# Weight preparation spread over a whole up-projection, five early loads, and a pending convolution in six steps

## The chip, the core and the metric

The kernel is one program on one core of a Trainium2 chip. The core has a matrix engine (TensorE, PE in the profile; its weight loads are the row PEld), VectorE (DVE), ScalarE (ACT), GpSimd (POOL), and SyncE (SP), whose queue issues nearly all transfers between the chip's memory (DRAM) and the on-chip buffers (SBUF). Matrix products are accumulated in PSUM, which DVE and ACT read. Each engine works through its own list of instructions in order, and waits on semaphores for the others. The metric is the time of one execution on the device in microseconds (us).

## What is computed

One layer on 2048 tokens of width 1024 in float32: an input projection, sparse indexed attention beside a pooling mixer, gates, an output projection, a layer norm, then the gated MLP that this study is about, and a second layer norm. The MLP, cut from the reference:

```python
D_MODEL, SEQ, D_FF, CONV_WIDTH = 1024, 2048, 2816, 3

def conv_ffn(x, conv_w, conv_b, w_up, w_down):
    h = x @ w_up
    h = lax.conv_general_dilated(h, conv_w[:, None, :], window_strides=(1,),
                                 padding=[(CONV_WIDTH - 1, 0)],
                                 dimension_numbers=('NWC', 'WIO', 'NWC'),
                                 feature_group_count=2 * D_FF) + conv_b
    gate, val = jnp.split(h, 2, axis=-1)
    return (jax.nn.silu(gate) * val) @ w_down

# in reference(), after the first layer norm:
ffn = conv_ffn(x, conv_w[l], conv_b[l], w_ffn_up[l], w_ffn_down[l])
x = layer_norm(ALPHA * x + ffn, ln2_g[l], ln2_b[l])
```

## The kernel before

**Arithmetic.** A float32 operand is split into a high part that the matrix engine takes as it is and a low part, the remainder. `mm3` then makes three matmuls of every product: high by high, high by low, low by high. The two big products of the MLP are made as 2 x 2 blocks by a scheme with seven block products instead of eight, so both operands are first added up into seven combinations, and the seven results are added up into the four blocks.

**Stages.** The program runs through projections, attention, the output projection with the first layer norm, and then `ffn`: `up_half(0)`, `down_half(0)`, `up_half(1)`, `down_half(1)`, one pair for each half of the tokens (1024). Work that is written out between two matmuls is put among the engines' lists by a scheduler, by the program's order and by what is ready.

**Up.** `up_half` has NF = 22 units, two for each of 11 channel groups (gate, then value). A unit makes seven products in the order ORDER, so a half has 154; each is 12 matmuls of 128x512. `evacuate` adds the results into the tiles h1 and h2. `conv` returns the causal convolution of a unit as six pieces (0 to 5): 0 and 1 are the three taps for h2, 2 and 3 for h1, and 4 and 5 (`hidden`) multiply value by gate and store two of the combinations for the down projection to DRAM (the tensors h). Each unit runs the pieces of the unit before it, one before each product; those of the last unit are left in `self.pending`. `hidden(1)` also queues five sums (`total`) in `self.hsum`; `self.hsum.pop(0)()` runs one at a time, and each is stored in h. They run on DVE in the first half, on POOL in the second.

**Weights of the up projection.** `up_weights` is a generator of 154 steps. A step makes one of the seven combinations of a unit's weights (a sum on POOL, except for two of seven; a high part by ACT; a low part on POOL) and stores it to DRAM (`uw`), at 512 KB. The first 98 steps (W_BEFORE = 14 units) run during attention. `up_more` runs the other 56 inside `up_half(0)`: W_RATE steps are credited for each product. `up_fetch` reads each weight back UP_AHEAD = 5 products before its use, in both halves. Stores go through `store`, which issues them a product or two later (`turn`). Stores and fetches are issued by SP, in one order.

**Down.** `down_half` makes seven products in the order DOWN, each of NP = 11 steps over p; a step is 4 row blocks of 3 matmuls of 128x512. Its operands are read by `down_load` (h from DRAM and one or two blocks of the weight, 256 KB each) and prepared by `down_split` (a sum on POOL where there are two blocks, the high part on ACT, the low part on DVE, or half on POOL). `loaded` and `split` count how far these are; a step splits two steps ahead and loads up to three further. `down_ahead` makes the first loads and splits inside the last unit of `up_half`. In the first steps, `down_half` runs the pending convolution and then the queued sums, and reads eight tiles of x. `lastk` holds the last steps of a product back and makes them row block by row block, so that `collect` (DVE, from PSUM) can start on the first block while PE does the others.

## Time and profile before

| | us |
|---|---|
| median of three timed runs | 3335.93 (3323.9 to 3339.29) |
| the profiled execution | 3325.95 |
| its span, from the first instruction to the last | 3324.2 |

The profile is of one execution. Its span is 1.75 us shorter than that execution's own time. In the trace, `up_half(0)` runs from about 1945 us to 2411 us, the down half after it to about 2640 us, the second up half to about 3090 us and the second down half to the end.

A row of a view by stretch gives the time from the start of the span, its length, and for each engine its busy time and, in brackets, how many instructions ran; then the granted clock of PE (1.00 is full speed), the mean busy share of the 16 DMA engines, and the rate in GB/s. In a view of waits, "A <- B: total, times, longest" says that engine A stood idle until B had released it. In a row of the timeline, the first two numbers are start and length, and in brackets at the end stands the idle time before it and what ended that. Names are the program's: b a large SBUF tile, m a half-size one, p PSUM, uw the prepared weights in DRAM, h the hidden combinations in DRAM, l a tile of the late pool. SPq is SP's queue, where a row is the issue of a transfer. Nearly every operation is recorded on the one line (L150) of a wrapper; of SP's lines, L363 is a store, L1471 a fetch of a weight, L1448 a load of raw up weights, L1617 and L1627 the loads of the down half, L1599 a store of h that is issued at once.

### The profile page before, as it was taken

To read this page: it belongs to the slowest core of one execution; us is meant where nothing else is said; L and a number is where in the kernel's file an instruction comes from. 1 tells how busy PE (TensorE), PEld (TensorE's weight loads), DVE (VectorE), ACT (ScalarE), POOL (GpSimd) and SP (SyncE) were. 2 spreads that over 40 slices of the span, in tenths; PEclk is the share of its full clock that TensorE was granted. 3 is DMA by queue.
4 is the path that set the end of the run, shared out by engine and by line. 5 is a ranking of instruction groups with operands and counts; after the bars stand their busy time and mean duration, and the time that the engine had idled before them with its cause. 6 is when DMAs were issued, how large, how long until landed. Compare 5 with 4: busy or idle time off the path is not lost. (4 is left out here: it accounts for less than half of the span.)

```text
span 3324.2 us, 46905 instructions
## 1 busy us (share of the span) xinstructions
PE 3168.4 (95%) x15918; PEld 2658.2 (80%) x15918; DVE 2423.5 (73%) x4475; ACT 1585.2 (48%) x2854; POOL 1271.3 (38%) x1302
## 2 busy tenths in 40 slices
PE   8998899999999899999999989999989999999898
PEld 8887688888898778888878877777868778888687
DVE  5589878996899887777676576666578765555597
ACT  3465737855678566666621133333244432223343
POOL 3139400010010787667731154550066511211684
PEclk9999899999999999999999999999999999999999
DMA  8457755754566344443464458997697665666884
GB/s 323 146 197 279 246 210 186 249 198 145 189 249 224 120 162 173 143 158 145 149 231 161 157 209 319 348 328 278 226 356 273 206 250 221 235 248 244 314 308 167
DMA packets 325679, 745.71 MB, mean 224 GB/s; under 512 B 30074, under 2 KB 115006, under 8 KB 325438
## 3 DMA queue, kind: packets, MB, share of 16 engines
q1 hardware_dynamic: 315646, 724.88, 60.8%
q10 hardware_dynamic: 9792, 17.83, 1.4%
q8 instruction: 126, 2.06, 0.3%
q14 instruction: 115, 0.94, 0.1%
HBM read 514.36 MB, written 228.23 MB: 223 GB/s over the span
## 5 line engine op out<-in xcount | busy, mean ns | idle before, releaser
L150 PE MATMUL p<-b,b 128*128 128x512 f32 (+3 forms) x12644 | 2785.6, 369 | 79.5 <-ACT b L150 20.6
L150 PEld LDWEIGHTS p<-b,b 128*128 128x128 f32 x12644 | 2173.6, 191 | 484.0 <-ACT b L150 23.1
L150 ACT ACTIVATE b<-p 128x512 fp32r<-128x512 f32 (+9 forms) x726 | 428.7, 612 | 667.9 <-PE p L150 628.1
L150 ACT ACTIVATE b<-b 128x1024 fp32r<-128x1024 f32 (+2 forms) x248 | 253.2, 1027 | 397.7 <-POOL b L150 148.9
L150 DVE TENSOR_TENSOR b<-b,b 128x1024 fp32r<-128x1024 f32 (+5 forms) x246 | 358.6, 1488 | 78.9 <-ACT b L150 75.9
L150 ACT ACTIVATE m<-b,F 128x448 bf16<-128x448 f32 (+3 forms) x448 | 366.1, 820 | 84.2 <-DVE F L150 67.3
L150 DVE TENSOR_SCALAR_CACHE_REDUCE m<-b,F 128x512 bf16<-128x512 f32 (+6 forms) x476 | 370.8, 808 | 17.8 <-DMA q<-m 12.4
L150 POOL TENSOR_TENSOR b<-b,b 128x256 fp32r<-128x256 f32 (+3 forms) x276 | 315.9, 1161 | 72.3 <-ACT b L150 66.2
L150 DVE TENSOR_TENSOR m<-m,p 128x512 f32<-128x512 f32 x176 | 120.5, 685 | 245.2 <-ACT b L150 207.0
L150 POOL TENSOR_TENSOR b<-b,m 128x512 f32<-128x512 f32 x110 | 196.7, 1808 | 237.9 <-DMA b<-h 165.3
L150 POOL TENSOR_TENSOR m<-b,b 128x512 f32<-128x512 f32 x99 | 144.4, 1466 | 349.4 <-issue 258.4
L150 DVE SCALAR_TENSOR_TENSOR b<-b,cw,b 128x1023 f32<-128x1023 f32 (+1 forms) x176 | 243.4, 1385 | 35.7 <-ACT b L150 34.5
L150 POOL TENSOR_SCALAR b<-b 128x256 fp32r<-128x256 f32 (+3 forms) x216 | 117.3, 558 | 379.4 <-DMA b<-in_w_in_dram 127.7
L150 PE MATMUL p<-b 128*128 128x512 f32 x616 | 235.8, 399 | 13.2 <-ACT b L150 8.7
L150 DVE TENSOR_TENSOR b<-p,b 128x512 fp32r<-128x512 f32 (+1 forms) x286 | 201.5, 713 | 59.5 <-ACT b L150 57.2
L150 PE MATMUL p<-ident,b 128*128 128x128 f32 x1456 | 214.8, 277 | 20.9 <-ACT b L150 14.4
L150 DVE CUSTOM_DVE_ANT_0 b<-p,b 128x1024 f32<-128x1024 f32 (+7 forms) x192 | 173.9, 908 | 67.4 <-PE p L150 66.1
L150 PEld LDWEIGHTS p<-ident,b 128*128 128x128 f32 x1456 | 176.6, 142 | 53.5 <-ACT b L150 17.5
L150 ACT ACTIVATE b<-b,mx 128x1024 f32<-128x1024 f32 (+7 forms) x192 | 171.6, 896 | 67.2 <-DVE mx L150 63.0
L150 DVE SCALAR_TENSOR_TENSOR b<-b,ws,b 128x768 f32<-128x768 f32 (+5 forms) x154 | 157.4, 1050 | 43.1 <-ACT b L150 41.0
L150 ACT ACTIVATE m<-p 128x512 f32<-128x512 f32 (+1 forms) x180 | 105.4, 593 | 152.9 <-PE p L150 136.9
L150 PE MATMUL p<-kst,b 128*128 128x384 f32 (+3 forms) x656 | 151.6, 361 | 4.5 <-DVE b L150 3.3
(126 smaller groups left out, 2386.7 us busy)
## 6 DMA issues: line engine op xcount, KB each, us to landing
b<-uw SPq DMA_DIRECT2D x308, 512.0 KB, 6.8
b<-wp SPq DMA_DIRECT2D x192, 512.0 KB, 6.2
uw<-l SPq DMA_DIRECT2D x98, 512.0 KB, 2.9
b<-in_w_ffn_down_dram SPq DMA_DIRECT2D x154, 256.0 KB, 5.4
b<-h SPq DMA_DIRECT2D x154, 256.0 KB, 5.4
wp<-b SPq DMA_DIRECT2D x64, 512.0 KB, 5.6
uw<-b SPq DMA_DIRECT2D x56, 512.0 KB, 5.4
h<-m SPq DMA_DIRECT2D x110, 256.0 KB, 5.6
```

The costliest lines, as they stand in the source:

```text
L150: return f(*args, **kw)
```

## The change

There are four edits, in numbers and in an index. W_RATE goes from 0.6 to 0.42: the 56 steps of weight preparation take 56/0.42 = 133 products instead of 56/0.6 = 93. DOWN_AHEAD = 5 loads (three before) and four splits (two before) are made in the last unit of each up half, from its third product on instead of its fifth. The pending convolution is run one piece in each of the first six steps of the down half, in the order 0, 1, 4, 2, 3, 5, instead of two pieces in each of three steps. In the sixth product of the first down half, three steps are held back instead of two.

```diff
--- before.py
+++ after.py
@@ -79,7 +79,8 @@
 W_PLAIN = {3: 0, 4: 3}
 W_SUMS = {2: (2, 3, OP.add), 1: (0, 3, OP.add), 6: (2, 0, OP.subtract), 5: (0, 1, OP.add), 7: (1, 3, OP.subtract)}
 UP_AHEAD = 5
-W_BEFORE, W_FROM, W_RATE = 14, 4, 0.6
+W_BEFORE, W_FROM, W_RATE = 14, 4, 0.42
+DOWN_AHEAD = 5
 DOWN = (4, 2, 1, 3, 6, 5, 7)
 H_PLAIN = {3: (0, 0), 4: (1, 1)}
 H_SUMS = {1: ((0, 0), (1, 1), OP.add), 2: ((0, 1), (1, 1), OP.add), 5: ((0, 0), (1, 0), OP.add),
@@ -1582,8 +1583,8 @@
                 else:
                     product(i, banks[BANK[m]], m, range(4))
                     evacuate(m, banks[BANK[m]], st)
-                if u == NF - 1 and s >= 4:
-                    self.down_ahead(hf, s - 4)
+                if u == NF - 1 and s >= len(ORDER) - DOWN_AHEAD:
+                    self.down_ahead(hf, s - len(ORDER) + DOWN_AHEAD)
                 yield 2.7
             pending = conv(st, n % 2, u // 2)
         self.pending = pending
@@ -1660,7 +1661,7 @@
         NP = NF // 2
         total = len(DOWN) * NP
         gb = self.load_norm("ln2_g", "ln2_b")
-        loaded, split = 3, 2
+        loaded, split = DOWN_AHEAD, DOWN_AHEAD - 1
         ys, fresh = {}, set()
 
         def product(acc, p, r, part):
@@ -1684,7 +1685,7 @@
                 t = [self.PS2([P, 2, G]) for _ in range(2)]
                 acc = [t[0][:, 0], t[0][:, 1], t[1][:, 0], t[1][:, 1]]
             final = hf == 1 and mi == len(DOWN) - 1
-            lastk = LASTK if final else 2 if hf == 0 and mi in (4, 5) else 0
+            lastk = LASTK if final else 2 if hf == 0 and mi == 4 else 3 if hf == 0 and mi == 5 else 0
             held = []
             for p in range(NP):
                 i = mi * NP + p
@@ -1698,9 +1699,8 @@
                 if loaded < min(split + 3, total):
                     self.down_load(hf, loaded)
                     loaded += 1
-                if mi == 0 and p < 3:
-                    self.pending[2 * p]()
-                    self.pending[2 * p + 1]()
+                if mi == 0 and p < 6:
+                    self.pending[(0, 1, 4, 2, 3, 5)[p]]()
                 elif self.hsum:
                     self.hsum.pop(0)()
                 if mi == 0 and 1 <= p <= 8:
```

The instructions are the same in kind and number on every engine; only their order changes. Three places show it. The first is SP's list in the middle of `up_half(0)`, from the fetch of weight 61 (uw_14179) to that of weight 67 (uw_14185). Rows b<-uw are fetches, rows uw<-b stores of prepared weights, h<-b is a store of h. Before:

```order
L1471 DMA b_23812<-uw_14179 128x1024
L1471 DMA b_23834<-uw_14180 128x1024
L363 DMA uw_14249<-b_23814 128x1024
L1471 DMA b_23853<-uw_14181 128x1024
L1471 DMA b_23877<-uw_14182 128x1024
L363 DMA uw_14250<-b_23855 128x1024
L1471 DMA b_23899<-uw_14183 128x1024
L363 DMA uw_14251<-b_23879 128x1024
L1471 DMA b_23918<-uw_14184 128x1024
L363 DMA h_186<-b_23817 128x512
L1471 DMA b_23941<-uw_14185 128x1024
L363 DMA uw_14252<-b_23920 128x1024
```

With the change:

```order
L1472 DMA b_23748<-uw_14179 128x1024
L1472 DMA b_23767<-uw_14180 128x1024
L1472 DMA b_23790<-uw_14181 128x1024
L364 DMA uw_14239<-b_23769 128x1024
L1472 DMA b_23810<-uw_14182 128x1024
L364 DMA uw_14240<-b_23812 128x1024
L1472 DMA b_23833<-uw_14183 128x1024
L1472 DMA b_23852<-uw_14184 128x1024
L1449 DMA b_23854<-in_w_ffn_up_dram 128x4x256
L1449 DMA b_23855<-in_w_ffn_up_dram 128x4x256
L364 DMA h_186<-b_23750 128x512
L1472 DMA b_23879<-uw_14185 128x1024
```

Between the same fetches stand two stores of weights instead of four, and the weights stored are ten earlier ones (121 and 122 instead of 131 to 134).

The second is SP's list at the last unit of `up_half(0)`, just behind the last fetches. Rows with in_w_ffn_down_dram are weight blocks for the down half (m: the second block of a sum), b<-h the hidden operand of the same load, h<-m the stores of sums of the hidden tiles. Before:

```order
L1471 DMA b_25700<-uw_14270 128x1024
L1471 DMA b_25722<-uw_14271 128x1024
L363 DMA h_236<-m_25724 128x512
L363 DMA h_247<-m_25744 128x512
L1617 DMA m_25800<-in_w_ffn_down_dram 128x512
L363 DMA h_258<-m_25764 128x512
L1617 DMA m_25820<-in_w_ffn_down_dram 128x512
L1617 DMA m_25843<-in_w_ffn_down_dram 128x512
L1617 DMA m_25861<-in_w_ffn_down_dram 128x512
L1617 DMA m_25871<-in_w_ffn_down_dram 128x512
L1617 DMA b_25799<-in_w_ffn_down_dram 128x512
L1627 DMA b_25799<-h_183 128x512
```

With the change:

```order
L1472 DMA b_25722<-uw_14271 128x1024
L364 DMA h_214<-m_25702 128x512
L1618 DMA b_25763<-in_w_ffn_down_dram 128x512
L1628 DMA b_25763<-h_183 128x512
L364 DMA h_236<-m_25724 128x512
L1618 DMA m_25764<-in_w_ffn_down_dram 128x512
L1618 DMA m_25789<-in_w_ffn_down_dram 128x512
L364 DMA h_247<-m_25744 128x512
L1618 DMA m_25815<-in_w_ffn_down_dram 128x512
L364 DMA h_258<-m_25769 128x512
L1618 DMA b_25788<-in_w_ffn_down_dram 128x512
L1628 DMA b_25788<-h_184 128x512
```

The first load's tile (b_25763) and its h now stand ahead of the stores h_236, h_247 and h_258, while before (b_25799) they stood behind them; the second load (b_25788) stands where the first stood before.

The third is DVE's list at the start of `down_half(0)`. Rows with cw are taps of the pending convolution, a TENSOR_TENSOR of 128x1024 from two other tiles is the low part of a split (or, where it writes its own first input, the product of value and gate), and m<-b,b is a queued sum. Before:

```order
L150 TENSOR_TENSOR b_25796<-m_25741,p_6505_25699 128x512
L150 TENSOR_TENSOR b_25867<-b_25842,b_25866 128x1024
L150 SCALAR_TENSOR_TENSOR b_25875<-b_25781,cw_22028,b_25875 128x1023
L150 SCALAR_TENSOR_TENSOR b_25875<-b_25781,cw_22028,b_25875 128x1022
L150 TENSOR_TENSOR b_25899<-b_25860,b_25898 128x1024
L150 TENSOR_TENSOR b_25875<-b_25875,b_25704 128x1024
L150 SCALAR_TENSOR_TENSOR b_25907<-b_25796,cw_22028,b_25907 128x1023
L150 TENSOR_TENSOR b_25928<-b_25870,b_25927 128x1024
L150 SCALAR_TENSOR_TENSOR b_25907<-b_25796,cw_22028,b_25907 128x1022
L150 TENSOR_TENSOR b_25907<-b_25907,b_25746 128x1024
L150 TENSOR_TENSOR b_25956<-b_25892,b_25955 128x1024
L150 TENSOR_TENSOR m_25964<-b_25907,b_25875 128x512
```

With the change:

```order
L151 TENSOR_TENSOR b_25869<-b_25839,b_25868 128x1024
L151 SCALAR_TENSOR_TENSOR b_25885<-b_25786,cw_22028,b_25885 128x1023
L151 SCALAR_TENSOR_TENSOR b_25885<-b_25786,cw_22028,b_25885 128x1022
L151 TENSOR_TENSOR b_25885<-b_25885,b_25704 128x1024
L151 TENSOR_TENSOR b_25923<-b_25862,b_25922 128x1024
L151 TENSOR_TENSOR b_25949<-b_25880,b_25948 128x1024
L151 SCALAR_TENSOR_TENSOR b_25957<-b_25811,cw_22028,b_25957 128x1023
L151 SCALAR_TENSOR_TENSOR b_25957<-b_25811,cw_22028,b_25957 128x1022
L151 TENSOR_TENSOR b_25976<-b_25900,b_25975 128x1024
L151 TENSOR_TENSOR b_25957<-b_25957,b_25746 128x1024
L151 TENSOR_TENSOR b_26002<-b_25926,b_26001 128x1024
L151 TENSOR_TENSOR m_26034<-b_25957,b_25885 128x512
```

The same six pieces are run ahead of the first queued sum. By then six splits had had their low part before, and now eight; the pieces of the two tiles (b_25885 and b_25957, before b_25875 and b_25907) have two splits between them, where before they followed each other directly.

## The prediction

> **What bounds the kernel now.** I began with the page's first part: the span, and who is busy in it.
>
> ```profile
> span 3324.2 us, 46905 instructions
> PE 3168.4 (95%) x15918; PEld 2658.2 (80%) x15918; DVE 2423.5 (73%) x4475; ACT 1585.2 (48%) x2854; POOL 1271.3 (38%) x1302
> ```
>
> PE is busy for 95%, so the end is set by PE's work, and a change that adds or removes no matmul (this one only moves work) can gain only where PE waits or runs at a low clock. The share is a mean over stages, so I next asked for busy times by stretch: the first up half while weights are still prepared, the rest of that half, the start of the first down half, then its middle, and the same pair for the second down half.
>
> ```profile
> core 0: us, PE busy (x) PEld busy (x) DVE busy (x) ACT busy (x) POOL busy (x), PEclk, DMA share, GB/s
> 1990.00:2260.00 270.00, 251.59 (x1045) 200.08 (x1046) 169.47 (x166) 93.81 (x151) 135.84 (x85) 0.96 0.94 338
> 2260.00:2405.00 145.00, 145.00 (x633) 117.61 (x632) 91.49 (x107) 43.68 (x60) 0.00 (x0) 1.00 0.63 233
> 2405.00:2475.00 70.00, 61.52 (x246) 45.95 (x246) 49.55 (x45) 26.98 (x28) 35.00 (x22) 0.98 0.94 343
> 3085.00:3155.00 70.00, 60.90 (x245) 47.36 (x244) 44.89 (x43) 26.76 (x26) 45.74 (x28) 0.95 0.91 326
> 3155.00:3300.00 145.00, 145.00 (x641) 120.10 (x640) 127.26 (x120) 66.17 (x70) 102.83 (x58) 1.00 0.76 265
> ```
>
> The number in brackets behind PE counts matmuls, so each row gives a pace. Undisturbed, the up half takes 145/633 = 0.229 us for one, or 2.75 us for a product of 12, and the down half 145/641 = 0.226 us. At these paces 1045 matmuls need 239.4 us of the first row's 270: **30.6 us are lost** while weights are prepared. The down starts need 55.6 and 55.4 of 70: **14.4 and 14.6 us** are lost. These three places hold nearly all that the change can touch.
>
> **Part 1: weight preparation at 0.42 steps for a product instead of 0.6.** Nothing is removed: 56 steps now take 133 products instead of 93, of 154. What ended PE's longest waits in the first row's stretch, what was transferred there (issues, size, us to landing), and whom the issuing queue (SP) waited for:
>
> ```profile
> PE p L150 <- DMA b<-uw: 14.0, 7, 4.6
> b<-uw SPq DMA_DIRECT2D x90, 512.0 KB, 6.8
> uw<-b SPq DMA_DIRECT2D x50, 512.0 KB, 5.4
> h<-m SPq DMA_DIRECT2D x30, 256.0 KB, 5.6
> b<-in_w_ffn_up_dram SPq DMA_DIRECT2D x12, 512.0 KB, 7.9
> h<-b SPq DMA_DIRECT2D x12, 256.0 KB, 6.3
> SPq L363 <- POOL b L150: 122.1, 42, 8.2
> ```
>
> PE waits seven times for a fetched weight (b<-uw). Two things make fetches late. First, bytes: 152 transfers of 512 KB (0.524 MB) and 42 of 256 KB are 90.7 MB; in 1045/12 = 87 products that is 1.043 MB each, which at 2.75 us a product asks for 380 GB/s, while the row shows 338 delivered at a DMA share of 0.94. 1.043 MB at 338 GB/s takes 3.09 us, just the pace seen (270/87 = 3.10). Second, order: SP issues in order and stood 122 us, 42 times, at a weight store whose POOL result was not ready, with fetches queued behind it. One such case, in order of time:
>
> ```profile
> 2058.16 0.62 SPq L1471 DMA_DIRECT2D b<-uw  x1
> 2067.05 0.32 SPq L363 DMA_DIRECT2D uw<-b  x1
> ...
> 2067.94 0.74 SPq L1471 DMA_DIRECT2D b<-uw  x1
> ...
> 2078.23 1.43 PE L150 MATMUL p<-b,b 128*128 128x512 f32 x5 [1.93 <-DMA b<-uw]
> ```
>
> Between two fetches lie 9.8 us in which SP waits for the store's data; the queue never recovers its lead and PE stands 1.93 us at 2078.
>
> At 0.42 the 50 stores and 12 loads of those 87 products become 35 and 8.4. Bytes: 90 x 0.524 + 35 x 0.524 + 8.4 x 0.524 + 42 x 0.262 = 80.9 MB, 0.930 MB a product, 338 GB/s at full pace: what the queues deliver today. So on average the loss by bytes goes to about nothing. Bounds: all 30.6 us at best; at worst the queues deliver only the 315 GB/s of the weakest 100 us of this stage, 2.95 us a product, 0.20 us lost in each of 133 products, 27 us, a gain of 4.
>
> ```profile
> 2000.00:2100.00 100.00, 92.56 (x387) 73.93 (x387) 63.50 (x62) 34.86 (x54) 54.91 (x33) 0.97 0.89 315
> 2100.00:2200.00 100.00, 94.76 (x406) 75.07 (x405) 68.32 (x69) 34.65 (x57) 49.34 (x33) 1.00 0.98 351
> ```
>
> I stay near the mean row (338), but bursts will leave some fetches late: a late fetch costs 30.6/7 = 4.4 us now with what follows it, the longer stretch has ten such places (133/87 of seven), and I leave two of them: 8.8 us remain, **gain 22 us**. POOL can keep up: its 85 operations were busy 135.84 of 270 us at 0.6 and have 1.4 times as long now. Weights are not late either: at product s, 98 + 0.42s are ready and s + 5 is fetched; the closest point is the last step, s = 133, where weight 153 is made 20 products before its use.
>
> The Trainium skill, DMA: Bandwidth & Descriptors, Specifications, gives about 358 GB/s of HBM for one core. As an estimate from that page, bandwidth then explains only 14 us of the 30.6 (87 products at 2.91 instead of 2.75 us); the rest would be order alone and stay, so the gain would be 14 and the sum below 8 us poorer, still inside the range. This trace's first row of the down start, further below, shows 399 GB/s over 5 us, so I don't take it as a ceiling.
>
> **Part 2: five loads and four splits of the down half inside the last unit, for three and two.** No instruction is added; two loads (3 x 256 KB each) and two splits (POOL sum, ACT high part, DVE low part) move ahead of the boundary. What PE waits for there now, in the first half and in the second:
>
> ```profile
> 2413.52 0.73 PE L150 MATMUL p<-b 128*128 128x512 f32 x2 [1.80 <-ACT b L150]
> 2414.94 1.39 PE L150 MATMUL p<-b,b 128*128 128x512 f32 x4 [0.69 <-DVE b L150]
> 2425.97 2.14 PE L150 MATMUL p<-b,b 128*128 128x512 f32 x8 [0.49 <-DVE b L150]
> 2430.53 2.11 PE L150 MATMUL p<-b,b 128*128 128x512 f32 x8 [1.50 <-DVE b L150]
> 2435.20 0.98 PE L150 MATMUL p<-b,b 128*128 128x512 f32 x3 [1.66 <-DVE b L150]
> ...
> 3098.42 2.08 PE L150 MATMUL p<-b 128*128 128x512 f32 x4 [2.43 <-ACT b L150]
> 3106.74 2.11 PE L150 MATMUL p<-b,b 128*128 128x512 f32 x8 [2.77 <-DVE b L150]
> 3125.67 2.03 PE L150 MATMUL p<-b 128*128 128x512 f32 x4 [2.58 <-ACT b L150]
> ```
>
> The first operand is split too late, since SP issues its loads only here:
>
> ```profile
> 2400.98 1.82 SPq L1617 DMA_DIRECT2D m<-in_w_ffn_down_dram  x1
> ```
>
> The change's order of SP puts the first load ahead of three of the stores on which SP stands, so it should leave some 5 us earlier; the other four leave 3 to 6 us earlier, since the buffers they fill come free only as PE finishes. All stay ahead of PE at 2.7 us a step, so the 1.80 + 0.69 us go, and with them the low clock behind them, 0.34 of 5 us = 1.7 us:
>
> ```profile
> 2410.00:2415.00 5.00, 2.51 (x11) 1.44 (x9) 1.50 (x2) 2.49 (x3) 2.54 (x2) 1.00 1.05 399
> 2415.00:2420.00 5.00, 5.00 (x15) 3.95 (x16) 5.00 (x5) 2.19 (x2) 2.22 (x2) 0.66 1.03 393
> 2425.00:2430.00 5.00, 3.53 (x15) 2.23 (x13) 5.00 (x4) 1.98 (x2) 2.06 (x1) 1.00 0.17 56
> ```
>
> The Trainium skill, TensorE: Matmul & The Clock Gate, HAM oscillation, warns of PE idle gaps over about 3.4 us. By it 1.80 and 0.69 us of idling cost no clock, and the sum would be 1.7 us poorer; the trace's clock fell all the same.
>
> The moved work needs cover: two splits are 2 x 1.365 us of DVE (mean of that operation below) in a last unit where DVE is busy 7.6 of 10 us and POOL idle. I cost them at nothing; without that cover it would be 2.7 us in each half.
>
> ```profile
> 2390.00:2400.00 10.00, 10.00 (x45) 8.04 (x44) 7.59 (x9) 5.13 (x6) 0.00 (x0) 1.00 0.34 137
> L150 DVE TENSOR_TENSOR b<-b,b 128x1024 fp32r<-128x1024 f32 (+2 forms) x24 | 32.4, 1365 | 16.2 <-ACT b L150 16.2
> L150 DVE SCALAR_TENSOR_TENSOR b<-b,cw,b 128x1023 f32<-128x1023 f32 (+1 forms) x4 | 7.1, 1764 | 0.0
> SPq L1599 <- DVE b L150: 10.8, 2, 7.8
> ```
>
> **Part 3: the pending convolution, one piece in each of six steps instead of two in each of three.** Same six pieces: 4 scalar_tensor_tensor of 1.76 us, 2 products, 2 or 4 ACT passes. Pressed into three steps (8 us) beside three splits they filled DVE (5.00 of 5 us at 2425), so both low parts and the h stores came late: SP stood 10.8 us in two waits at such stores, and DMA fell to a share of 0.17 at 2425. Spread over six steps, with two splits in hand, DVE has about 16 us for them. What is late next is the five sums behind it, now in steps 6 to 10 instead of 3 to 7; the first one's store is read at step 16, ten steps (27 us) on: no cost. In the second half those sums run on POOL, beside the splits' own sums, and the 2.58 us wait at 3125 may stay in part.
>
> Parts 2 and 3 together, first half: 2.5 + 1.7 (boundary and clock) plus 0.49 + 1.50 + 1.66 = 7.9 us at stake in these rows, bounds 3 and 12; I take **7**. Second half: 2.43 + 2.77 + 2.58, and 0.05 x 70 = 3.5 us of clock, 11.3 at stake, bounds 3 and 12.5; I take **8**.
>
> **Part 4: three held steps instead of two in one product of the first down half.** PE waits for DVE's collection at the next product:
>
> ```profile
> PE p L150 <- DVE b L150: 4.5, 2, 2.8
> 2615.00:2620.00 5.00, 3.34 (x8) 2.16 (x8) 5.00 (x8) 0.00 (x0) 3.64 (x3) 0.50 1.07 348
> ```
>
> 4.5 us of waits and 2.5 us of clock: 7 us at most. The first block's sums end one step's 0.68 us x 3 = 2 us earlier, but DVE is full (5.00 of 5) and blocks two to four collect as before. I take **1.5**, bounds -1 (buffers held longer) and 7.
>
> **Sum.** 22 + 7 + 8 + 1.5 = 38.5 us. The profiled execution took 3325.95 us, so 3287.5 on its terms. The median of the three timed runs is 3335.93, 10 above; the mean of all four is 3331.3. A median of new runs stands nearer to that mean, so I add 5.3: **3293 us**.
>
> **Rivals.** *The transfers stay late* (part 1 gains 4): for it, 338 GB/s asked of queues that give 338 on average; against it, the heaviest 100 us of this stage (351 GB/s, share 0.98) had PE idle 5.2 us, the lighter ones before (315) 7.4, so the queues can give more than 338. 3331.3 - 20.5 = 3311. *The loads don't really leave earlier* (the change doesn't do what it says): the second to fifth still stand behind the same h stores in SP's order, and parts 2 and 3 give 2.5 in all. 3331.3 - 26 = 3305. *Both*: 3323. *Slower*: what is lost goes with products passed beside weight stores, not with their density. SP waited 122.1/42 = 2.9 us for a store here, and nearly the same, 214.2/72 = 3.0, in attention, where stores come sparsely:
>
> ```profile
> SPq L363 <- POOL l L150: 214.2, 72, 11.6
> ```
>
> If each product beside preparation goes on losing 30.6/87 = 0.35 us, 40 more of them cost 14 us, and SP standing at h stores keeps the down starts as they are: 3331 + 14 = 3345. It decides if fetches are issued less than 8 us before use as often as now. Against it: the bytes alone give today's pace to 0.01 us.
>
> **How the numbers follow.** Forecast 0.60; loads not earlier 0.13; transfers late 0.13; both 0.05; slower 0.04; all at their best ends (gain near 60) 0.05. A measurement of this kernel tells about 0.5% (17 us) from no change. Below 3319 lie the forecast, the best case, the loads' rival and half of the transfers' rival and more: faster 0.85, same 0.11, slower 0.04. The range runs from the best case, 3272, to just past the transfers' rival, 3316.
>
> **What would show it.** Right: PE's waits for b<-uw fall from seven to about two, their stretch now reaching to about 2340 with a DMA share near 0.9 and 340 GB/s; no wait over 1 us at either boundary; 246 matmuls in the first down start in 60 us, not 70. Wrong: SP's waits for POOL over 3 us each with PE idle behind them past 2260; first loads of the down half issued no earlier than 12 us before the boundary; DVE full and PE waiting in steps 6 to 10.

## The result and the profile after

The changed kernel took **3290.75 us** (median of four runs, 3282.79 to 3297.32) against 3336.11 for the kernel before (four runs): a ratio of **0.987**, with a 95% interval of 0.9837 to 0.9903. 3293 us were forecast, in a range of 3272 to 3316. The profiled execution took 3290.62 us. The total agrees with the forecast to 2 us. Runs of one kernel lie 15 us apart here, so an agreement as close as that is luck; the profiled pair gained 35.3 us, where 38.5 were forecast. The parts are another matter, as the runs below show.

The profiled execution's span is 3288.8 us. Who is busy in it, from the first part of the page after (busy us, share of the span, instructions):

```profile
PE 3150.3 (96%) x15918; PEld 2650.6 (81%) x15918; DVE 2439.5 (74%) x4475; ACT 1581.9 (48%) x2854; POOL 1263.1 (38%) x1302
```

PE has the same 15918 matmuls and is busy 18 us less: stretches in which the granted clock was 0.50 became rarer. The stretches that answer to those of before, in the windows of the profile after (from:to, length, then busy us and instructions of each engine, PE's clock, the DMA engines' share, GB/s):

```profile
1990.00:2260.00 270.00, 261.26 (x1129) 210.00 (x1128) 180.82 (x182) 92.33 (x149) 103.65 (x67) 1.00 0.91 325
2260.00:2405.00 145.00, 141.61 (x609) 114.44 (x608) 95.07 (x100) 51.70 (x75) 41.83 (x29) 0.99 0.87 313
2385.00:2455.00 70.00, 64.94 (x280) 52.00 (x280) 56.98 (x51) 30.19 (x31) 41.88 (x26) 1.00 1.01 373
3050.00:3120.00 70.00, 67.02 (x285) 54.12 (x284) 52.32 (x48) 29.21 (x29) 49.86 (x31) 0.98 1.00 361
```

In 270 us of weight preparation PE now gets 1129 matmuls done, not 1045; in the 145 us behind, 609, not 633, since preparation reaches into them.

Equal times hold different work, so the comparisons from here on are cut **by place**: from the start of one matmul to the start of a later one, counted from the program's beginning, which are the same two places in every kernel. (The count in brackets includes the one that begins at the cut.) Three places are used: 1749 of the first up half's 1848 matmuls (this is what the expectations below call the first up half; undisturbed, at the forecast's 0.229 us, it needs 400.5 us), 260 around the first down start, and 290 around the second. The same windows view, before:

```profile
1964.32:2407.36 443.04, 415.63 (x1750) 332.44 (x1749) 280.28 (x289) 146.53 (x225) 152.27 (x105) 0.97 0.83 302
2407.36:2480.71 73.35, 64.86 (x261) 48.76 (x260) 50.36 (x46) 28.14 (x28) 40.71 (x26) 0.98 0.95 349
...
3079.83:3160.60 80.77, 71.67 (x291) 56.11 (x290) 49.63 (x47) 30.76 (x30) 52.95 (x32) 0.96 0.91 325
```

and after:

```profile
1968.19:2392.45 424.26, 408.18 (x1750) 328.02 (x1749) 282.48 (x290) 145.36 (x228) 152.61 (x108) 0.99 0.89 317
2392.45:2457.06 64.61, 60.27 (x261) 48.49 (x260) 54.67 (x47) 29.19 (x28) 43.26 (x26) 1.00 1.04 391
...
3054.00:3125.27 71.27, 68.29 (x291) 55.36 (x290) 55.92 (x48) 30.27 (x30) 54.69 (x32) 0.98 1.01 369
```

The three places gave 18.8, 8.7 and 9.5 us. Of the first one's 18.8, 7.4 are PE's busy time (415.63 to 408.18, clock 0.97 to 0.99) and the rest is waits. What ended PE's waits in that stretch (us in total, times, longest), before:

```profile
PE p L150 <- DMA b<-uw: 14.0, 7, 4.6
PE p L150 <- DVE m L150: 6.5, 3, 5.0
PE p L150 <- DVE b L150: 5.6, 4, 2.5
```

and after:

```profile
PE p L151 <- DVE b L151: 8.3, 5, 2.4
PE p L151 <- DVE m L151: 6.2, 4, 4.0
PE p L151 <- DMA b<-uw: 1.5, 2, 0.8
```

Waits for fetched weights (b<-uw) nearly vanish, seven to two, as foretold. What is left are waits for DVE, 14.5 us in nine against 12.1 in seven before, which the forecast had not reckoned with. And SP, whose standing at weight stores was the forecast's second reason for late fetches, stands there longer than ever, 134.7/34 = 4.0 us each, against 2.9 before (SP's waits, after, 1990 to 2260 us):

```profile
SPq L364 <- POOL b L151: 134.7, 34, 8.0
```

At the boundaries it went as the forecast said. The first loads of the down half leave SP at 2372 us, 24.5 us ahead of the down half's first matmul (2396.57), where before the first left at 2400.98, 12.5 us ahead of 2413.52 (SP's timeline, after). The last transfer of that first load follows at 2381 us, where before it left at 2406, so the load as a whole leaves nearly 8 us earlier against the boundary; some 5 were foretold.

```profile
2372.04 0.39 SPq L1618 DMA_DIRECT2D b<-in_w_ffn_down_dram  x1
```

No wait over 1 us stands at either boundary. Behind the first stay one of 2.19 us at a distance of 27 us and one of 1.07 us at 36; behind the second stays one of 2.85 us at 31, where ACT waits for the splits' sums on POOL (PE's and ACT's rows in the timeline after):

```profile
2423.33 2.14 PE L151 MATMUL p<-b,b 128*128 128x512 f32 x8 [2.19 <-DVE b L151]
```

```profile
3091.27 3.90 ACT L151 ACTIVATE b<-b 128x1024 fp32r<-128x1024 f32 x4 [9.33 <-POOL b L151]
...
3092.38 1.20 PE L151 MATMUL p<-b 128*128 128x512 f32 x4 [2.85 <-ACT b L151]
```

### The profile page after: what moved, and what is told of

Its sections match the earlier page's. It is cut to its first block, busy times and chain, and to the rows that moved or that the text cites. A ratio compares the mean times of both kernels' runs of the same rounds, so it can differ in the third digit from the quotient of the medians.

```text
span 3288.8 us, 46936 instructions
## 1 busy us (share of the span) xinstructions
PE 3150.3 (96%) x15918; PEld 2650.6 (81%) x15918; DVE 2439.5 (74%) x4475; ACT 1581.9 (48%) x2854; POOL 1263.1 (38%) x1302
## 5 line engine op out<-in xcount | busy, mean ns | idle before, releaser
L151 PEld LDWEIGHTS p<-b,b 128*128 128x128 f32 x12644 | 2170.6, 191 | 455.9 <-ACT b L151 24.5
L151 ACT ACTIVATE b<-b 128x1024 fp32r<-128x1024 f32 (+2 forms) x248 | 253.4, 1027 | 386.7 <-POOL b L151 132.1
L151 DVE TENSOR_TENSOR b<-b,b 128x1024 fp32r<-128x1024 f32 (+5 forms) x246 | 365.9, 1523 | 50.2 <-ACT b L151 47.9
L151 DVE TENSOR_SCALAR_CACHE_REDUCE m<-b,F 128x512 bf16<-128x512 f32 (+6 forms) x476 | 370.7, 808 | 13.9 <-DMA q<-m 10.5
L151 ACT ACTIVATE b<-b,mx 128x1024 f32<-128x1024 f32 (+7 forms) x192 | 171.5, 896 | 68.2 <-DVE mx L151 63.5
```

The lines of the kernel that those rows point to most:

```text
L151: return f(*args, **kw)
```

## The experiments: the parts alone

Part 1, part 2, and parts 3 and 4 together were put into the kernel before, and the kernel before was profiled once more.

**Before, again** (no edit).

> The kernel before, unchanged, profiled once more, to see how far two profiles of one kernel differ stage by stage. Between the two profiles shown, the first 109 matmuls of the first up half (some 25 us) got 8.3 us shorter after the change, which my forecast didn't count, and the program ahead of it 3.9 us longer. If the 8.3 is the change's work, this profile repeats the slow start within 2 us; if it is scatter, it moves by 4 us or more.

Measured 3330.88 us; the windows of this second profile:

```profile
1969.60:2413.32 443.72, 417.24 (x1750) 333.93 (x1749) 280.56 (x289) 146.53 (x226) 150.22 (x105) 0.96 0.83 302
2413.32:2486.01 72.69, 64.80 (x261) 48.69 (x260) 50.30 (x46) 28.11 (x28) 41.07 (x26) 0.98 0.94 344
...
3085.87:3165.53 79.66, 72.05 (x291) 55.70 (x290) 49.43 (x47) 30.66 (x30) 51.73 (x32) 0.96 0.93 330
```

443.72 for 443.04, 72.69 for 73.35, 79.66 for 80.77: these two profiles of one kernel agree to about 1 us by place. The first 109 matmuls of the stretch took 39.35 and 39.44 us, and 31.07 after, so those 8.3 us are the change's work. What lies ahead of the up half moved by 5.3 us between these two profiles of one kernel; that is scatter, and so are the 3.9 us there after the change.

**Part 1 alone**, the rate:

```
-W_BEFORE, W_FROM, W_RATE = 14, 4, 0.6
+W_BEFORE, W_FROM, W_RATE = 14, 4, 0.42
```

> Before with part 1 alone (0.42 weight steps for a product). My theory: the whole gain of the first up half, about 19 us, comes from here, PE waits for fetched weights (b<-uw) in two or three places instead of seven, and both down starts stay as before within 2 us; time about 3317, ratio 0.994. Rival (the early loads of part 2 also relieve SP's queue in the late up half): the up half gains 12 us or less, or a down start moves by over 4 us.

3313.34 us, ratio 0.9953 (0.9936 to 0.997). Its windows:

```profile
1971.78:2394.26 422.48, 407.90 (x1750) 327.95 (x1749) 280.07 (x289) 144.24 (x226) 149.88 (x106) 0.99 0.88 316
2394.26:2467.23 72.97, 63.87 (x261) 47.34 (x260) 50.78 (x46) 28.27 (x28) 41.20 (x26) 1.00 0.95 345
```

The up half gets all its gain from the rate (20.6 us; one wait for a fetched weight is left, 0.4 us), and the down start stays. The rival is out.

**Part 2 alone**, five loads and four splits:

```
-                if u == NF - 1 and s >= 4:
-                    self.down_ahead(hf, s - 4)
+                if u == NF - 1 and s >= 2:
+                    self.down_ahead(hf, s - 2)
...
-        loaded, split = 3, 2
+        loaded, split = 5, 4
```

> Before with part 2 alone (five loads and four splits ahead, convolution still two pieces in each of three steps). My theory: the boundary waits and the low clock behind them go, 4 us in the first down start and 3 in the second, while the waits in the steps behind, where DVE is full of convolution pieces, stay; about 7 in all, time about 3329, ratio 0.998. Rival one (the loads alone are the cure): 8 us or more in the first down start with no wait over 1 us left. Rival two (the convolution alone is the cause): under 1.5 us in each.

3323.43 us, ratio 0.9975 (0.9962 to 0.9988). Its windows:

```profile
2411.15:2478.64 67.49, 63.05 (x261) 49.34 (x260) 45.46 (x45) 27.14 (x27) 40.73 (x25) 0.97 0.97 357
...
3077.85:3153.21 75.36, 70.23 (x291) 54.88 (x290) 51.33 (x47) 29.54 (x29) 50.62 (x31) 0.98 0.94 343
```

5.9 and 5.4 us: more than the 4 and 3 of my theory, less than the 8 of the first rival. The work moved ahead of the boundary, which the forecast cost at nothing, shows as about 1 us: the last 640 of the up half's 1749 matmuls took 148.1 us, against 147.05 before, with PE idle for 0.9.

**Parts 3 and 4 alone**, the convolution in six steps and three held steps:

```
-                if mi == 0 and p < 3:
-                    self.pending[2 * p]()
-                    self.pending[2 * p + 1]()
+                if mi == 0 and p < 6:
+                    self.pending[(0, 1, 4, 2, 3, 5)[p]]()
...
-            lastk = ... 2 if hf == 0 and mi in (4, 5) else 0
+            lastk = ... 2 if hf == 0 and mi == 4 else 3 if hf == 0 and mi == 5 else 0
```

> Before with part 3 alone (the pending convolution in six steps) and part 4 (three held steps), which lie 130 us apart, so that each is read at its own place. My theory: the waits behind the boundary go (3 to 4 us in the first down start, 4 to 5 in the second), the first one, where PE waits for a late split at the boundary, stays; part 4 gives 1 us or less. Time about 3328, ratio 0.998. Rival: with only two splits ahead the six steps do nothing, under 1.5 us in each start.

3325.86 us, ratio 0.9987 (0.9975 to 0.9999). Its windows (the third is the place of part 4, 250 matmuls around the last product but one and the half's end):

```profile
2418.54:2488.13 69.59, 62.35 (x261) 49.26 (x260) 52.24 (x46) 29.10 (x28) 43.02 (x26) 0.98 0.98 362
2599.95:2663.44 63.49, 56.24 (x251) 45.09 (x250) 49.62 (x51) 29.54 (x42) 35.92 (x23) 0.95 0.71 236
3087.56:3165.42 77.86, 71.01 (x291) 55.91 (x290) 61.24 (x48) 32.61 (x32) 55.47 (x34) 0.96 0.96 354
```

3.8 and 2.9 us at the starts, the second below the 4 to 5 expected: with only two splits ahead the six steps are worth something, but less than part 2. By place the parts about add up, 9.6 and 8.3 us against 8.7 and 9.5 together. The timed runs can't confirm it: the three ratios alone make 0.85%, or 28 us, and the whole change 1.3%, or 43 us, with intervals that overlap. In this kernel the first up half, in which nothing is changed, took 445.48 us, so single profiles scatter there by 2 us or more. Part 4's place took 63.39 us before, 63.92 in its second profile and 63.49 here: nothing by itself.

## The experiments: what makes the up half slow

The forecast's first part had a mechanism, bytes first and SP's order second. Seven kernels test it, and an eighth tries another cure; all are made from the changed kernel, and all but the eighth ran once.

**Two other rates**, 0.50 and 0.40 in the line above.

> The changed kernel with 0.50 weight steps for a product instead of 0.42: the same 56 steps over 112 products. Read by place, from the first matmul of the first up half to its last: before 443.1 us, after 424.3. By bytes (0.980 MB a product asks 356 GB/s, 338 were delivered at 0.6) each of the 112 products loses 0.15 us, 17 us in all, so this lies between the two, near 433. By order alone (the loss comes from the number of products passed beside stores) 21 fewer products make it a little shorter than after, about 420.

> The changed kernel with 0.40 steps for a product, over 140 products. By bytes (0.918 MB, 334 GB/s asked) nothing more is to be had: 424 us within 3 for the first up half. If each product beside stores costs 0.35 us, 7 more cost 2.4. If density still bites, it gets shorter by 3 us or more.

3307.58 and 3295.55 us. The up half took 425.45 us at 0.40, and at 0.50, in the windows view:

```profile
1973.04:2404.49 431.45, 411.01 (x1750) 331.22 (x1749) 287.48 (x290) 143.74 (x224) 158.21 (x106) 0.98 0.87 313
```

443 us at 0.6 (the kernel before), then 431, 424 and 425 at 0.5, 0.42 and 0.40: the fewer steps in a time, the less is lost, down to about 0.42. The bytes theory foretold both figures to 2 us. That proves little, for bytes, POOL's work, ScalarE's copies and SP's stores all thin out together with the rate; the next kernels part them.

**Order without bytes**: 0.6, each weight's store handed over one weight step later.

```
+                if inside:
+                    held.append((self.d_w[n * len(ORDER) + s], t.bitcast(F32)))
+                    if len(held) > 1:
+                        self.store(*held.pop(0))
+                else:
                     self.store(self.d_w[n * len(ORDER) + s], t.bitcast(F32))
```

> The changed kernel at the old 0.6 steps, but each weight's store is handed to SP's queue one weight step later, when POOL has long made it: the same bytes at the same density, without SP standing at the stores. By order: SP's waits for POOL at the weight stores fall from 2.9 us each to under 1, PE's waits for fetched weights go, and the first up half takes about 425 us. By bytes: SP's waits fall just so, but the queues are as full, PE waits for fetched weights as before, and the half takes 440 or more.

3316.01 us. Its window and what PE waited for there:

```profile
1970.09:2415.90 445.81, 415.63 (x1750) 333.37 (x1749) 285.30 (x290) 147.55 (x226) 158.22 (x106) 0.97 0.82 302
```

```profile
PE p L151 <- DVE b L151: 17.4, 7, 4.1
PE p L151 <- DVE m L151: 6.4, 3, 5.8
PE p L151 <- DMA b<-uw: 5.6, 3, 3.1
```

Neither theory had this. SP stood for POOL at the stores only 20 times in 300 us instead of 46 times, though still for 2.6 us each and not under 1, and the waits for fetched weights fell from 14.0 to 5.6 us. So order has a part in the late fetches, unless it was the waits for DVE that gave them time. For PE now waited for DVE, 17.4 us instead of 5.6, and nothing was gained: something else was as late as the fetches.

**Bytes without order**: 0.42, and one more load of 256 KB a weight step.

```
                 self.store(self.d_w[n * len(ORDER) + s], t.bitcast(F32))
+                if inside:
+                    nc.sync.dma_start(self.M([P, G]), self.a["w_ffn_down"][0, :P, :G])
```

> The changed kernel at 0.42, with one more load of 256 KB at each weight step inside the first up half, whose data nobody reads: 1.04 MB a product again, the stores as sparse as in the change. By bytes: 0.3 us lost in each of 133 products, PE waits for fetched weights more often than the two times of after, and the first up half takes 440 us or more, up to 460. By order: the stores and SP's waits at them are as in the change, so it stays at 424 within 4.

3297.94 us. Its windows, the second of them 140 us in the middle:

```profile
1963.98:2395.33 431.35, 410.35 (x1750) 329.56 (x1749) 284.42 (x290) 146.72 (x227) 150.08 (x108) 0.99 0.94 346
```

```profile
2100.00:2240.00 140.00, 135.85 (x587) 108.83 (x586) 89.29 (x92) 46.85 (x73) 50.88 (x33) 1.00 0.98 363
```

**The bytes theory's ceiling falls here.** In the second row 363 GB/s were delivered, 50.8 MB in 587/12 = 49 products, 1.04 MB a product, just what before asked for; and the products took 2.86 us, not 3.10. The half lost 7 us of the 18.8, not the 16 to 36 foretold, and PE waited for a fetched weight once, 2.9 us. By place the loss lies in the half's first 109 matmuls (36.40 us, 31.07 in the change) and its last 640; the 1000 between them took 239.30 us, 240.65 in the change. Whether bytes cost those 7 us is open, since each added load also takes a tile of the pool m, which the evacuations use. But the 338 GB/s of before were what was asked at the pace that PE kept, not what the queues could give; the change's own row of the first down start, further above, has 391. One reserve: the added load reads the same block each time, and whether other bytes are as cheap wasn't tried.

So a new theory: the weight steps hold up the engines that empty PE's banks. Three kernels test whose work it is.

**ScalarE out of the steps**, at 0.6:

```
+                if inside:
+                    u, v, op = W_SUMS.get(m, (0, 3, OP.add))
+                    nc.gpsimd.tensor_tensor(t[:, 0], a[u], a[v], op=op)
+                    nc.gpsimd.tensor_tensor(t[:, 1], a[u], t[:, 0].bitcast(F32), op=OP.subtract)
```

> The changed kernel at 0.6 again, with ScalarE out of the weight steps: inside the first up half the high part of a weight is written by POOL's sum itself, and its low part is not the true one (the two plain products in seven get a sum as well, so POOL has 2 operations a step instead of 1.7). Bytes, stores and their number as before. First up half: before 443 us, after 424. A new theory after the late stores and the filler moved it little: the weight steps share engines with the evacuations. If it is ScalarE's copies, on which POOL's low parts and DVE's convolution wait in turn, the half falls to 430 or less; if it is POOL's work, which slows DVE (its 128x1022 pass took 1.66 us here before and 1.28 in the second up half, where no weights are made), or bytes, it stays at 437 or more.

3319.19 us; 447.60 us for the stretch, with waits for DVE of 18.3 and 8.9 us:

```profile
1968.69:2416.29 447.60, 413.00 (x1750) 331.50 (x1749) 289.30 (x290) 119.83 (x173) 187.41 (x123) 0.97 0.82 302
```

With ScalarE's copies gone, and POOL with 17% more operations, the half is no faster. Nothing here speaks for the copies, but POOL was also busy for 167.11 of 270 us instead of 135.84, which can hide a small gain.

**POOL out of the steps**, at 0.6:

```
+                if inside:
+                    nc.scalar.activation(t[:, 0], a[0], AF.Copy)
+                    nc.scalar.activation(t[:, 1], a[3], AF.Copy)
```

> The changed kernel at 0.6 with POOL out of the weight steps of the first up half: ScalarE copies a loaded block into each half of the weight (the sums and the low parts are left out), two copies a step instead of one; bytes, stores and their number as before. If POOL's work beside DVE is the cause: DVE's 128x1022 pass falls to about 1.3 us, PE's waits for fetched weights and for DVE go, and the first up half takes 412 us or less (its 1749 matmuls at 0.229 us are 400.5). If ScalarE's copies are the cause: 443 or more. If bytes: 437 or more.

3311.99 us. Its window and DVE's second convolution pass (from the groups of DVE, 1990 to 2260 us: count, busy us, mean ns):

```profile
1974.43:2408.42 433.99, 413.90 (x1750) 331.38 (x1749) 249.49 (x288) 173.66 (x278) 5.67 (x13) 0.98 0.85 308
```

```profile
L151 DVE SCALAR_TENSOR_TENSOR b<-b,cw,b 128x1022 f32<-128x1022 f32 x25 | 32.0, 1281 | 0.6
```

DVE is back at 1.28 us as foretold, but the half takes 434 us, not 412: half of the gain, at 0.6 and with every byte in place. PE still waits five times for fetched weights (9.3 us), and nearly as long for DVE as before, 10.0 us in eight against 12.1 in seven, where these waits were expected to go. SP now stands at the stores for ScalarE, which makes both halves.

**More POOL work**, at 0.42:

```
+                if inside:
+                    nc.gpsimd.tensor_tensor(self.M([P, 4, P]), a[0], a[3], op=OP.add)
```

> The changed kernel at 0.42 with one more POOL sum of 128x512 behind each weight step inside the first up half, whose result nobody reads: POOL's work in time as dense as at 0.6, the bytes, stores and ScalarE's copies as sparse as in the change. If POOL's work beside DVE is the cause, the first up half goes back to 435 us or more and DVE's 128x1022 pass to 1.6 us or more. If it is bytes, or ScalarE's copies, it stays at 424 within 4.

3312.56 us. The same two views:

```profile
1969.66:2412.53 442.87, 416.50 (x1750) 333.15 (x1749) 309.54 (x290) 145.78 (x227) 253.42 (x164) 0.97 0.85 304
```

```profile
L151 DVE SCALAR_TENSOR_TENSOR b<-b,cw,b 128x1022 f32<-128x1022 f32 x25 | 47.2, 1887 | 0.6
```

All of the gain is gone (442.87 for 443.04 before), with no byte and no store added. The dose was larger than meant: an added sum takes 1.8 us, and POOL is busy 169.57 of the 270 us from 1990 to 2260 where before it was 135.84. So more work on POOL is enough to lose it all. The added sum takes a tile of the pool m as well, but so did the added load above, which lost only 7 us. This run doesn't say by which way POOL's work reaches PE (later stores or a slower DVE: PE's waits for fetched weights rose from 1.5 to 5.4 us, those for DVE from 14.5 to 20.9), nor that it acted alone before.

**Other pairs of banks**, in the changed kernel. In odd units the four PSUM banks are two tiles of two:

```
-                banks = [t[0][:, 0], t[0][:, 1], t[1][:, 0], t[1][:, 1]]
+                banks = [t[0][:, 0], t[1][:, 0], t[0][:, 1], t[1][:, 1]]
```

> The changed kernel with the two-bank PSUM tiles of the odd units paired otherwise: banks 0 and 2 in one tile and 1 and 3 in the other, instead of 0 with 1 and 2 with 3. Bytes, stores, POOL's and ScalarE's work are those of the change. In the trace after, PE waits every 40 us at the last of an odd unit's products for DVE, since that product writes into the same tile as the product right ahead of it and so waits for that one's evacuation; in the new pairing one more product lies between. If DVE's late evacuations are what is left to wait for, those waits (DVE b: 8.3 us in five, from 1964 to 2400 us) fall under 2 us, the first up half from 424 to 417 to 420 us, and the time to about 6 us below the change's, 3285, ratio to before 0.985. Rival: DVE is late for all that follows as well, the wait only moves one product on, and the half stays at 424 within 2.

3282.30 us, ratio 0.9853 (0.9836 to 0.9869): the fastest kernel of the study, though its interval overlaps the change's; this one ran four times. By place, the stretch and, further on, 1550 matmuls of the second up half:

```profile
1973.17:2387.94 414.77, 402.86 (x1750) 328.47 (x1749) 278.27 (x290) 145.19 (x228) 151.82 (x107) 1.00 0.90 324
```

```profile
2660.14:3013.04 352.90, 352.90 (x1551) 290.92 (x1550) 199.07 (x281) 99.74 (x112) 56.61 (x45) 1.00 0.66 249
```

9.5 us better than the change in the first, against 4 to 7 foretold, and 3.3 in the second, where the change took

```profile
2660.99:3017.21 356.22, 356.22 (x1551) 288.84 (x1550) 197.40 (x281) 99.62 (x112) 56.61 (x45) 1.00 0.65 246
```

The reason was only half right: waits for DVE b stay at 7.2 us in five, where under 2 was expected, so DVE is late for the product behind as well. The second half has no wait in either kernel; there PE simply runs at 0.2277 instead of 0.2298 us a matmul. An estimate from these two paces is that 3.7 us of the first stretch's 9.5 (1749 matmuls) are pace too, and no wait. In the old pairing matmuls of an odd unit stand in a mixed order: around 2709 us of the trace after, seven with one operand from the late pool are followed by twelve others and then by two more of the seven's kind, while in the new kernel, around 2710 us, nine of that kind stand in one piece. That the order causes the better pace is likely but wasn't tried by itself, and why the scheduler mixes them isn't shown.

## Why the prediction was right in sum, and where it was wrong

**Where time was lost**: right. All that the change gained by place lies where the forecast named it: 18.8, 8.7 and 9.5 us in the three stretches and 2.3 at part 4's place make 39.3, of which the scatter ahead of them took 3.9; the spans differ by 35.4.

**Part 1, "gain 22"**: 18.8 us here and 20.6 with the rate alone, but this is not the forecast's 22. It counted from 1990 us on and left out the half's start. From the matmul that begins there (1990.60 us before, 1988.44 after) to the end of the stretch the gain is 12.8 us (416.76 to 404.01); the other 6.0 came ahead of it (26.28 to 20.25). The mis-sized term is "I leave two of them: 8.8 us remain": two late fetches did remain, at 1.5 us, but 404.01 - 1686 x 0.229 = 17.9 us are still lost. The term put all 30.6 us down to seven late fetches, whose own waits were 14.0 us, and none to DVE, for which PE waited 7.1 us in the same 270; after, 10.5 of the 12.0 us of waits from 1990 us on are for DVE. An error of 9 us and one of 6 nearly cancelled, which is luck.

**The step that failed** is the mechanism: "1.043 MB at 338 GB/s takes 3.09 us, just the pace seen". That agreement was a coincidence or rather a circle: bytes in a window divided by its time give its rate, whatever limits it. With the same bytes a product, the filler's run delivered 363 GB/s. The second reason, order, isn't enough by itself: with it mostly gone, PE waited for DVE at 0.6, and the half took as long. What the forecast said of POOL, that it "can keep up", was true of its own time and left out what it does to the others: with more POOL work at 0.42 all of the gain was gone. DVE's 128x1022 pass, which doesn't touch PSUM, took 1.66 us before, 1.53 after, 1.28 with POOL out and 1.89 with more POOL; here in the groups of before and after (1990 to 2260 us), beside the pass that adds a PSUM bank:

```profile
L150 DVE SCALAR_TENSOR_TENSOR b<-b,cw,b 128x1022 f32<-128x1022 f32 x25 | 41.5, 1660 | 0.6
...
L150 DVE TENSOR_TENSOR m<-m,p 128x512 f32<-128x512 f32 x50 | 34.2, 684 | 80.8 <-ACT b L150 58.2 <-PE p L150 22.6
```

```profile
L151 DVE SCALAR_TENSOR_TENSOR b<-b,cw,b 128x1022 f32<-128x1022 f32 x27 | 41.3, 1530 | 0.7
L151 DVE TENSOR_TENSOR m<-m,p 128x512 f32<-128x512 f32 x54 | 36.7, 683 | 77.8 <-ACT b L151 46.2 <-PE p L151 24.2 <-POOL m L151 7.3
```

How PE comes to wait for DVE is seen once in 40 us; the timeline after, in order of time (start, us, and in brackets the idle time ahead and who ended it):

```profile
2106.21 1.28 DVE L151 SCALAR_TENSOR_TENSOR b<-b,cw,b 128x1022 f32<-128x1022 f32 x1
2107.58 1.06 ACT L151 ACTIVATE b<-b 128x1024 f32<-128x1024 f32 x1 [7.06 <-DVE b L151]
2108.55 1.23 ACT L151 ACTIVATE b<-b,cw 128x1024 f32<-128x1024 f32 x1
...
2109.80 1.28 DVE L151 SCALAR_TENSOR_TENSOR b<-b,cw,b 128x1023 f32<-128x1023 f32 x1 [2.32 <-ACT b L151]
2110.37 1.85 POOL L151 TENSOR_TENSOR b<-b,b 128x512 fp32r<-128x512 f32 x1 [8.23 <-ACT b L151]
2111.01 0.68 DVE L151 TENSOR_TENSOR b<-m,p 128x512 f32<-128x512 f32 x1
2111.60 1.70 DVE L151 SCALAR_TENSOR_TENSOR b<-b,cw,b 128x1022 f32<-128x1022 f32 x1
...
2111.74 2.34 PE L151 MATMUL p<-l,b 128*128 128x512 f32 x9 [2.37 <-DVE b L151]
```

DVE and ACT take turns: DVE's pass, ACT's gate, ACT's next first pass, DVE's pass, and only behind it the evacuation (2111.01) for which PE stands 2.37 us. POOL waited 8.23 us in this chain too, for a copy behind ACT's, so its store comes late and SP stands. The 128x1022 pass took 1.28 us with POOL idle and 1.70 beside it, five microseconds later. But that longer pass stands behind the evacuation, and both passes ahead of it took 1.28, so POOL lengthened nothing that this wait rests on. Such waits come without it, too: with POOL out, PE's waits for DVE are 2.58 us at 2082.00 and 1.82 at 2124.97. So that more POOL work slows the half is shown; that it does so by way of DVE's longer passes is not.

What it was at 0.6 stays open. Over the half, taking POOL out gave about 9 us of 18.8 and putting the bytes back cost 7, which nearly fills the sum, but by place it doesn't. Of the 18.8 us, 16.0 were gained in the 1000 matmuls behind the first 109, and there no single part explains them:

| kernel | first 109 matmuls, us | next 1000, us |
|---|---|---|
| before, and its second profile | 39.4, 39.4 | 256.6, 257.2 |
| the change | 31.1 | 240.7 |
| 0.6, late stores | 39.5 | 259.3 |
| 0.6, ScalarE out | 40.5 | 260.1 |
| 0.6, POOL out | 32.6 | 253.4 |
| 0.42, bytes put back | 36.4 | 239.3 |
| 0.42, more POOL work | 34.5 | 255.0 |

In the 1000, bytes cost nothing, POOL out gave 3 to 6 us, and late stores or ScalarE out gave none. Either several of these hold up the pace at once, so that taking out one leaves the others, or the cause is something else that thins with the rate. Each row is one profile, and there is none of the changed kernel with only the old rate; the kernels with parts 2 to 4 alone, at 0.6, took 259.3 and 259.7 us there, and 447.1 and 445.5 for the half. Taking POOL out and delaying the stores together, which would say what the five fetch waits left in the POOL-less kernel are, wasn't tried.

**Parts 2 and 3, "7" and "8"**: 8.7 and 9.5 in the profiled pair. All nine profiles at hand with both parts take 64.6 to 68.0 us at the first start and 71.0 to 72.5 at the second, against 72.7 to 73.4 and 79.3 to 80.8 in the three profiles with neither: right in place and, with means of 6.5 and 8.1 us over these profiles, in size; the place and kind of the waits agree with the mechanism. One term was put at nothing without being nothing: the five queued sums, now in steps 6 to 10 of the first down half. There PE waits 3.3 us for DVE (0.73, 0.34 and 2.19 us, from 2414 to 2424), which is busy 13.55 of the 16 us from 2412; the forecast had named this as a sign of being wrong. The wait near 3125, said to "stay in part" because of POOL's sums, is still there whole, 2.85 us for 2.58.

**Part 4, "1.5"**: not shown. Its place took 63.5 us alone, 63.4 to 65.0 without it, and 60.6 to 62.9 where all parts are in; about 1.5 may be there, but only beside the others.

**The rivals.** That transfers stay late fell with the fetch waits; that loads don't leave earlier fell with the 24.5 us; that each product beside stores loses 0.35 us fell at 0.42 and 0.40. Its sign, SP standing over 3 us a store, did come true, 4.0 us, while PE's waits for fetched weights fell to 1.5 us all the same: how long a queue stands says little without what it had to bring next.

## What to carry to other kernels

A rate worked out as bytes over time, in a stretch where something waits, is what was asked for, not what can be had: before calling it a ceiling, add bytes and look. When background work is spread thinner everything about it thins together, so a right forecast of the time proves no mechanism; take its parts out one at a time, read the result by place, and where no single part brings the time back, take out two. And how PSUM banks are paired in tiles is worth a trial: here pairing banks that are used two products apart instead of back to back gave 9.5 us in 424, though not by the way that was expected.

## What the runs showed of the hardware

**POOL's work lengthens DVE's passes that read two operands from SBUF, and not those with one operand in PSUM.** Over the kernels above, 1.28 us (POOL out) to 1.89 us (densest POOL) for 128x1022, while the pass with one operand in PSUM took 0.68 to 0.69 us in each of them. The Trainium skill, SBUF — State Buffer, SBUF: two separate sides, says why: DVE instructions with two SBUF inputs and GpSimd's share a pair of ports, which one holds for a whole instruction while the other stands. The trace agrees on which passes suffer. By that rule the pass at 2111.60 above should have stood until POOL's operation ended at 2112.22, 0.62 us; it grew by 0.42, which is near, POOL's spans being rough.

**This core's DMA queues gave 363 GB/s over 140 us** (the filler's run, share 0.98) with PE at 97% and full clock, 25 more than before in its fullest 270. The change's row of the first down start, further above, shows 391 over 64.6 us.
